# Low-rank and bonus products of an RWKV-7 step in two passes of rounded parts, with the bonus kept in DRAM

## The chip, the cores and the metric

The kernel runs on one core of one Trainium2 chip. The metric is the device time of one execution in microseconds; lower is better. The core has a matmul engine (TensorE, PE), a vector engine (VectorE, DVE), a scalar engine (ScalarE, ACT), GpSimd (POOL) and a sync engine (SyncE, SP) that issues most of the DMAs. Each engine works through its own queue in order and waits on semaphores of the others.

## The reference

One inference step of a hybrid decoder layer, 512 prompt tokens and 8 x 8 sample tokens (576 columns in all), width 1024. RWKV-7 time mixing and differential attention run on the same normalised input, are merged by gates, and a squared-ReLU MLP follows. What matters here is the RWKV branch, 8 heads of 64, cut to the lines that the change computes:

```python
r, k, v, wd, ad, gd = jnp.split(Pr, RWKV_SPLITS, axis=-1)   # wd, ad: 64 wide
w = -jax.nn.softplus(-(lp['w0'] + jnp.tanh(wd) @ lp['w2']).astype(f32)) - 0.5
a = jax.nn.sigmoid((lp['a0'] + ad @ lp['a2']).astype(f32))
g = jax.nn.sigmoid(gd) @ lp['g2']
...
S, y = rwkv7_scan(S0, hs(r), hs(decay), hs(k), hs(v), -kk, kk * hs(a))
...                                                          # y: group norm per head
bonus = jnp.sum(hs(r) * hs(k) * lp['r_k'], axis=-1, keepdims=True) * hs(v)
o = (y + bonus).reshape(B, T, W_A) * g
```

The decay w and the rate a come from products of rank 64 (`w2`, `a2`); the bonus is a sum over the 64 channels of a head, times v.

## The kernel before, in words

Activations lie with channels on the 128 partitions and the 576 tokens along the free axis, split in halves of 288 (`HALF`) for matmuls. Large projections (`stream`) multiply in three passes of rounded parts: the weights and the activations are each split into a rounded high part (an ACT copy to fp32r) and a low part (a DVE subtraction), and high x high, high x low and low x high are summed in PSUM. Their weights come in by SP's queue as tiles `raw_*` (`raw_z` for the RWKV projections, `raw_g` for the gates, `raw_brb`, `raw_bra`, `raw_wo`, `raw_dn` later).

The RWKV projections `shifted(0..13)` give the tiles `Pt[i]`: r, k, v of each of four head pairs hp, then `Pt[12]`, whose lower 64 partitions are wd and upper 64 ad, and `Pt[13]`, gd. After the attention, its pool `ap` closes, and the pools `rb_` and `rt` for the heads open in the space that it leaves. Tiles of the tag "T" in `rt` are 128x576, and six of them exist at a time; a new one waits until one is released.

The generator `rwkv(hp)` does a head pair in stages between its `yield`s:

- Stage 0: `sq`, the squares of k, are summed on PE (`pn`, tiny products), turned into inverse norms on POOL (`nr`, then `nb`), and spread by PE transposes (`pk`). Decay and rate are matmuls `pw` and `pa` of full fp32 operands: `wl` and `al` are 128x512 tiles, zero in the half of the partitions that belongs to the other, so that each multiplies all of `Pt[12]`. ACT empties them by tanh into `u` and `aa`. DVE makes the running sums `cum`, ACT the exponentials `pe`, `pinv`, `pm`. Then come the mixed keys `k2`, `rkp` (r k r_k), the bonus sums `pbn` (an fp32 matmul with a block of ones), `bv` (the bonus times v, a tile of `rb_` with four buffers, kept on chip until the norm), the operands `KB` and `ST`, and the intra-chunk products `pA` with masks (`ABR`, `ST`).
- Stages 1 to 3: transposes, sample states (`s0`, loaded by SP; `pI`), the triangular inverse by 32x32 blocks (`pW`, `pZ`), sample outputs (`pF`). `chain(0)` and `chain(1)` run the nine chunks of two pairs in series (`pch`, `pY`).
- Stage 4: mean and variance of y, the power on POOL. Stage 5: scaling, transposes (`pTy`), `oa` = normed y times weight plus bias, plus `bv`, times the gate `pg`.

Work that fills PE between these steps is taken from a list, `waiting`: the projections of the next pairs (`ps_z`), the gates (`ps_g`), and branch B's output products (`ps_brb`), in amounts written out by hand (`fill(8)`, `take(221)` and so on). `fill` also binds the work to come after the last matmul on PE. Every instruction has a priority, its place in the program unless `prio` gives another, and the order on each queue is planned from these and from when tiles come free; weight loads and their splitting stand ahead of all else (`FEED`). Branch B loads `ob` and `gb` tiles, also of the tag "T"; so are `y2` of the last two pairs and the `g` tiles of the last stage of the branch.

Of the kernel before, what the change touches and what calls it, by code (L numbers as in the profile page):

```python
# [8 lines left out]
F32 = mybir.dt.float32  # L9
F32R = mybir.dt.float32r  # L10
I32 = mybir.dt.int32
AF = mybir.ActivationFunctionType
# [3 lines left out]
P = 128  # L16
# [5 lines left out]
NT = NPR + NS  # L22
# [19 lines left out]
def tile_hybrid_step(ctx, tc, xT, xsT, ktab, vtab, s0T, ptab, w_in, vecs, w2a2, g2, lamv,  # L42
                     w_bra, w_brb, w_out, w_up, w_down, cst, bias_p, bias_s,
                     yT, kTo, vTo, Sp, Ss, sh):
    nc = tc.nc
    PE, VE, AE, GE = nc.tensor, nc.vector, nc.scalar, nc.gpsimd
    PS = bass.MemoryType.PSUM

    def pool(name, bufs=1, stack=ctx, **kw):
        return stack.enter_context(tc.tile_pool(name=name, bufs=bufs, **kw))  # L50

    def f32(ap):
        return ap.bitcast(F32)
# [3 lines left out]
    def act(out, in_, func=AF.Copy, **kw):  # L57
        ring["act"] = AE.activation(out=out, in_=in_, func=func, **kw)  # L58

    def tt(out, a, b, op, eng=None):  # L60
        ins = (eng or VE).tensor_tensor(out=out, in0=a, in1=b, op=op)  # L61
        if eng is None:
            ring["tt"] = ins

    def stt(out, a, s, b, op0, op1):
        VE.scalar_tensor_tensor(out=out, in0=a, scalar=s, in1=b, op0=op0, op1=op1)

    def ts(out, a, s1, op0, s2=None, op1=ALU.bypass, eng=None):
        (eng or VE).tensor_scalar(out=out, in0=a, scalar1=s1, scalar2=s2, op0=op0, op1=op1)

    def mm(out, lhsT, rhs, start=True, stop=True):
        ring["mm"] = PE.matmul(out=out, lhsT=lhsT, rhs=rhs, start=start, stop=stop)  # L72
        return ring["mm"]
# [17 lines left out]
    MUL, ADD, SUB, MAX = ALU.mult, ALU.add, ALU.subtract, ALU.max  # L91
# [9 lines left out]
    def bank(name):  # L101
        return psw.tile([P, 512], F32, tag="w", name=name)

    def tbank(name):
        return psc.tile([P, 512], F32, tag="t", name=name)
# [9 lines left out]
    onesblk = c[:, C_OB:C_OB + P]  # L115
# [13 lines left out]
    up = tbank("warmup")  # L129
# [4 lines left out]
    def v(i, n=1):  # L134
        return vec[:, i:i + n]
# [88 lines left out]
    def fill(n):  # L224

        with tc.issue_after(ring["mm"].ins):
            take(n)
# [12 lines left out]
    def rpow(dst, src, scale, eps):  # L240

        ts(dst, src, scale, MUL, eps, ADD)
        GE.tensor_tensor(out=dst, in0=dst, in1=mhalf[:dst.shape[0], :dst.shape[1]], op=ALU.pow)
# [17 lines left out]
    rc = pool("rc", stack=ph1)  # L261
# [5 lines left out]
    zp = pool("zp", stack=ph1)  # L267
# [3 lines left out]
    with tc.tile_pool(name="xin", bufs=2, reuse_waits="tile") as xin:  # L271
# [6 lines left out]
        for k in range(0, KT, 4):  # L278
            for j in range(3):
                with prio(FEED + 1000 + 10 * k + j):  # L280
                    name = f"raw_{'qkv'[j]}0_{k}"
                    if k == 0:
                        raw = ring["pool"].tile([P, 4, P], F32, tag="raw", name=name, bufs=3)
                    else:
                        raw = zw.tile([P, 1 + NX], F32, tag="z" if j else "tz", name=name,
                                      bufs=2 if j else 1)[:, :4 * P].rearrange("p (k w) -> p k w", k=4)
# [25 lines left out]
    Pt = [None] * 14  # L312
# [5 lines left out]
    ts(ka2[:, 0:4], v(V_KA, 4), 0.5, MUL, 0.0, ADD, GE)  # L318
    ts(ka2[:, 4:8], v(V_KA, 4), -0.5, MUL, 1.0, ADD, GE)

    wl = rc.tile([P, 512], F32, name="wl")
    al = rc.tile([P, 512], F32, name="al")
    GE.memset(wl[64:128], 0.0)
    GE.memset(al[0:64], 0.0)
    wg = rc.tile([P, 512], F32, name="wg")
    reset = rc.tile([P, NT], F32, name="reset")
    GE.memset(reset, 1.0)
# [87 lines left out]
    with tc.issue_after(behind.ins):  # L415
        nc.sync.dma_start(out=pti, in_=ptab)
        nc.sync.dma_start(out=lv, in_=lamv)
        nc.sync.dma_start(out=bp, in_=bias_p)
        nc.sync.dma_start(out=bs, in_=bias_s)
        nc.sync.dma_start(out=wl[0:64], in_=w2a2[0:64])  # L420
        nc.sync.dma_start(out=al[64:128], in_=w2a2[64:128])
        nc.sync.dma_start(out=wg, in_=g2)

    def shifted(i):
# [240 lines left out]
    for h in range(HB):  # L665
        if h:
            qkv(h)
        for cc in range(2):
            GE.tensor_copy(
                out=qbd[64 * cc:64 * cc + 64, :, h, 8 * cc:8 * cc + 8],  # L670
                in_=qT[64 * cc:64 * cc + 64, h, NPR:].rearrange("p (b q) -> p b q", b=NB))
# [11 lines left out]
    while flight:  # L683
        feed()
        fill(8)
    act(Pt[12][0:64], Pt[12][0:64], AF.Tanh)
    sg = Pt[13]
    act(sg, sg, AF.Tanh, scale=0.5)
    ts(sg, sg, 0.5, MUL, 0.5, ADD)
# [25 lines left out]
    rk = ExitStack()  # L715
    rb_ = pool("rb_", 2, stack=rk, reuse_waits="tile")
    rt = pool("rt", 2, stack=rk, reuse_waits="tile")

    def ch(a):
        return a.rearrange("p (c t) -> p c t", t=64)  # L720
# [21 lines left out]
    def rwkv(hp):  # L742
        e = hp % 2
        own = pair.setdefault(hp // 2, {})
        hs = slice(hp * P, (hp + 1) * P)
        r, k, vv = Pt[hp], Pt[4 + hp], Pt[8 + hp]

        def tmp(tag, bufs=1):
            return rt.tile([P, NT], F32, tag="T", name=f"{tag}_{hp}", bufs=6)
# [5 lines left out]
        for t, o in enumerate(toks):  # L755
# [8 lines left out]
                       in_=nr.rearrange("p (a o) -> p a o", o=1).broadcast_to([P, 10, 64]))  # L764
        u = tmp("u")
        aa = tmp("aa")
        for t0, n in HALF:
            pw = bank(f"pw{hp}{t0}")
            mm(pw[:, :n], wl[:, hs], Pt[12][:, t0:t0 + n])
            act(u[:, t0:t0 + n], pw[:, :n], AF.Tanh, scale=0.5, bias=hw0[:, hp:hp + 1])  # L770
            pa = bank(f"pa{hp}{t0}")
            mm(pa[:, :n], al[:, hs], Pt[12][:, t0:t0 + n])
            act(aa[:, t0:t0 + n], pa[:, :n], AF.Tanh, scale=0.5, bias=hw0[:, 4 + hp:5 + hp])
        (fill if hp != 2 else take)(8)
        ts(u, u, 1.0, ADD)
# [25 lines left out]
        tt(k2, k2, k, MUL)  # L801
        rkp = tmp("rkp")
        stt(rkp, r, v(V_RK + hp), k2, MUL, MUL)
        bv = rb_.tile([P, NT], F32, tag="bv", name=f"bv{hp}", bufs=4)
        for t0, n in HALF:
            pbn = bank(f"pbn{hp}{t0}")
            mm(pbn[:, :n], onesblk, rkp[:, t0:t0 + n])
            tt(bv[:, t0:t0 + n], pbn[:, :n], vv[:, t0:t0 + n], MUL)


        KB = rt.tile([P, NCH, 2, 64], F32, tag="KB", name=f"KB{hp}", bufs=1)
# [14 lines left out]
        for par in range(2):  # L826
            rows = slice(64 * par, 64 * par + 64)
# [15 lines left out]
        for cs, pV in two_chunks(f"pV{hp}", vv):  # L843
            for a, c0, c1 in cs:
                src = pV[64 * a:64 * a + 64].rearrange("p (c w) -> p c w", w=P)[:, :(c1 - c0 + 1) // 2]
# [20 lines left out]
        for par in range(2):  # L866
            rows = slice(64 * par, 64 * par + 64)
# [29 lines left out]
        for l in range(1, 5):  # L897

            n = NCH if l < 3 else 8
# [55 lines left out]
        var = stat.tile([P, NCH], F32, tag="var", name=f"var{hp}")  # L955
        VE.tensor_reduce(out=var, in_=y2, axis=AX.X, op=ADD)
        rpow(var, var, 1.0 / 64, 64e-5)

        yield
        tt(y, y, b9(var), MUL)  # L960
# [3 lines left out]
        for cs, pT_ in two_chunks(f"pTy{hp}", y.rearrange("p c t -> p (c t)")):  # L964
            for a, c0, c1 in cs:
                src = pT_[64 * a:64 * a + 64].rearrange("p (c w) -> p c w", w=P)[:, :(c1 - c0 + 1) // 2]
# [78 lines left out]


    gens = [rwkv(hp) for hp in range(4)]

    def run(*stages):
# [254 lines left out]
    rows = []  # L1304
# [10 lines left out]
    for t0, n in LAST:  # L1315
# [55 lines left out]
        w = slice(0, len(tiles))  # L1371
# [133 lines left out]
```

## Time and profile before

| | |
|---|---|
| median of 3 runs | 1001.76 us (1001.45 to 1002.26) |
| profiled execution: span, first to last instruction | 1004.0 us; no other time of it is given |
| busy: PE, DVE, ACT, POOL | 975.5, 689.5, 497.3, 88.3 us |
| share of PE in the chain that ended last | 86% |
| mean granted TensorE clock | 0.989 |

Busy time is the time in which an engine had an instruction at work; a matmul's end is modelled, and matmuls overlap, so their start-to-start distance is what a row of them costs. A row of a timeline gives start, length, engine, line, operation, tile written <- tiles read, shapes and a count. A bracket at its end gives the idle time of that engine before it and what ended it. The head pairs run from about 172 to 522 us.

### The profile page before, as it was taken

Reading aid. Unit: us, or ns where it says so; the run is one execution under the profiler, and the core shown is the slowest. Engines: PE = TensorE matmul, PEld = TensorE weight load, DVE = VectorE, ACT = ScalarE, POOL = GpSimd, SP = SyncE. Lnnn points to the kernel's source line nnn. Section 1 sums busy time; section 2 is a strip of 40 time slices with the busy share of each in tenths; the row PEclk is TensorE's granted clock in tenths of the full one; section 3 lists DMA queues with packets and bytes.
Section 4 is the critical chain, followed back from the end, with each engine's and each line's share of the span. In section 5 each row is a group of like instructions: output and inputs, shape, how many; then the busy total and the mean of one; then the engine's idle time right before and its main releaser. Section 6 shows DMA issues by size and latency. Waiting matters only on the chain.

```text
span 1004.0 us, 24422 instructions
## 1 busy us (share of the span) xinstructions
PE 975.5 (97%) x10012; PEld 919.9 (92%) x10012; DVE 689.5 (69%) x1459; ACT 497.3 (50%) x1094; POOL 88.3 (9%) x171
## 2 busy tenths in 40 slices
PE   8999999899999999999999999999999999999996
PEld 8999998898887878888889999999999999999996
DVE  6698666774946669445588798966666666666744
ACT  6576555354435344443344666644444444444732
POOL 2511001301010340000300000000000000000001
PEclk9999999999989989999999999999999999999998
DMA  7312673121111225222377642222222222221402
GB/s 265 142 66 88 204 221 120 54 64 45 43 47 57 69 87 171 80 70 102 106 215 237 195 152 74 95 85 95 85 85 95 84 85 85 85 84 44 128 10 95
DMA packets 50833, 105.75 MB, mean 105 GB/s; under 512 B 6066, under 2 KB 8114, under 8 KB 50594
## 3 DMA queue, kind: packets, MB, share of 16 engines
q1 hardware_dynamic: 47442, 96.95, 30.2%
q0 software_dynamic: 1648, 5.35, 1.4%
q8 instruction: 79, 1.29, 0.5%
q10 hardware_dynamic: 1632, 1.89, 0.5%
q14 instruction: 32, 0.26, 0.1%
HBM read 89.38 MB, written 14.78 MB: 104 GB/s over the span
## 4 chain that ended last, share of the span: by engine, by line
PE 86%; DVE 6%; ACT 3%; DMA 2%; issue 2%; POOL 1%; SPq 0%; DVEq 0%; POOLq 0%; ACTq 0%
PE ps_dn L72 21%; PE ps_g L72 9%; PE ps_z L72 8%; PE ua L1224 5%; PE ux L1224 5%; PE ps_wo L72 4%; PE uc L1224 3%; PE ud L1224 3%; PE ub L1224 3%; PE ps_k L72 2%; PE ps_brb L72 2%; PE pch L72 2%; PE ps_q L72 2%; PE ps_v L72 2%; PE pA L72 2%
## 5 line engine op out<-in xcount | busy, mean ns | idle before, releaser
L72 PE MATMUL ps_dn<-q,hi_dn 128*128 128x288 f32 x768 | 154.7, 296 | 0.0
L72 PEld LDWEIGHTS ps_dn<-q,hi_dn 128*128 128x128 f32 x768 | 122.8, 188 | 1.5
L72 PE MATMUL ps_dn<-q,lo_dn 128*128 128x288 f32 x384 | 113.2, 295 | 0.0
L72 PE MATMUL ps_g<-xl,hi_g 128*128 128x288 f32 x256 | 80.2, 313 | 0.0
L72 PE MATMUL ps_g<-xh,lo_g 128*128 128x288 f32 x256 | 79.3, 310 | 0.0
L72 PE MATMUL ps_g<-xh,hi_g 128*128 128x288 f32 x256 | 79.2, 310 | 0.0
L72 PEld LDWEIGHTS ps_dn<-q,lo_dn 128*128 128x128 f32 x384 | 72.1, 188 | 0.0
L72 PE MATMUL ps_z<-xh,lo_z 128*128 128x288 f32 (+1 forms) x224 | 69.6, 311 | 0.0
L72 PE MATMUL ps_z<-xh,hi_z 128*128 128x288 f32 (+1 forms) x224 | 68.3, 305 | 0.0
L72 PE MATMUL ps_z<-xl,hi_z 128*128 128x288 f32 (+1 forms) x224 | 67.6, 302 | 0.0
L61 DVE TENSOR_TENSOR ya<-ya,ps_dn 128x288 f32<-128x288 f32 x96 | 43.4, 453 | 29.3 <-PE ps_dn L72 29.3
L58 ACT ACTIVATE hi_dn<-raw_dn 128x512 fp32r<-128x512 f32 x48 | 30.1, 628 | 57.0 <-PE ps_dn L72 57.0
L1224 PE MATMUL ua<-h_b,hi 128*128 128x288 f32 x256 | 53.2, 298 | 0.0
L1224 PE MATMUL ux<-h_t,hi 128*128 128x288 f32 x256 | 52.3, 296 | 0.0
L58 ACT ACTIVATE c<-c 128x288 f32<-128x288 f32 x112 | 48.4, 439 | 7.5 <-DVE c L61 5.8
L72 PEld LDWEIGHTS ps_g<-xh,hi_g 128*128 128x128 f32 x256 | 49.0, 191 | 2.9 <-issue 1.6
L72 PEld LDWEIGHTS ps_g<-xl,hi_g 128*128 128x128 f32 x256 | 49.0, 191 | 1.9
L72 PEld LDWEIGHTS ps_g<-xh,lo_g 128*128 128x128 f32 x256 | 49.1, 192 | 1.4
L58 ACT ACTIVATE hi<-a 128x1024 fp32r<-128x1024 f32 (+1 forms) x32 | 27.1, 846 | 42.0 <-PE ps_dn L72 34.3
L72 PE MATMUL ps_dn<-q,w 128*128 128x320 f32 (+1 forms) x336 | 46.4, 298 | 0.0
L61 DVE TENSOR_TENSOR lo<-s,hi 128x1024 fp32r<-128x1024 f32 x32 | 39.2, 1225 | 10.2 <-ACT hi L58 10.0
L72 PEld LDWEIGHTS ps_dn<-q,w 128*128 128x128 f32 x336 | 45.3, 190 | 0.1
(395 smaller groups left out, 2801.7 us busy)
## 6 DMA issues: line engine op xcount, KB each, us to landing
a<-in_w_up_dram SPq DMA_DIRECT2D x32, 512.0 KB, 3.3
raw_dn<-in_w_down_dram SPq DMA_DIRECT2D x64, 256.0 KB, 2.9
raw_g<-in_w_in_dram SPq DMA_DIRECT2D x32, 256.0 KB, 3.2
raw_z<-in_w_in_dram SPq DMA_DIRECT2D x28, 256.0 KB, 3.0
gt_d<-gg SPq DMA_DIRECT2D x16, 288.0 KB, 2.5
g<-gt_d SPq DMA_DIRECT2D x16, 288.0 KB, 3.7
kp<-in_ktab_dram SPq DMA_DIRECT2D x16, 256.0 KB, 4.0
vp<-in_vtab_dram SPq DMA_DIRECT2D x16, 256.0 KB, 3.7
```

The costliest lines, as they stand in the source:

```text
L58: ring["act"] = AE.activation(out=out, in_=in_, func=func, **kw)
L61: ins = (eng or VE).tensor_tensor(out=out, in0=a, in1=b, op=op)
L72: ring["mm"] = PE.matmul(out=out, lhsT=lhsT, rhs=rhs, start=start, stop=stop)
L1224: ring["mm"] = PE.matmul(out=ps[:, :288], lhsT=l[:, k], rhs=hb[blk][:, h, k], start=start and i == 0, stop=i == 11, skip_group_check=skip)
```

## The change

The low-rank products and the bonus sums are made of rounded parts in two passes each.

- One tile `wa` holds both weights, w2 on partitions 0 to 63 and a2 on 64 to 127; `wl`, `al` and their two memsets go, and two DMAs become one.
- After the pools `rb_` and `rt` open, the weights of each are rounded to `hi` (twice, into both halves of the partitions) and the remainder goes to `lo` (also into both). `stacked` puts the rounded activation on the rows of its own half and its remainder on the other half's, so that one pass with `hi` gives high x high plus high x low, and a second with `lo` adds low x high (and low x low). `xa` is made of ad; the tanh of wd, before done in place after the projection, goes to a tile `th` here, and `xw` is made of that.
- `pw` and `pa` become two fp32r matmuls each (`lowrank`).
- `rkp` is split into `rkh` (ACT) and `rkl` (DVE), and the bonus sum is two fp32r matmuls with `ones2`, a rounded copy of the block of ones.
- `bv` becomes a tile of the tag "T", is written to DRAM (`bv_d`) by SP's queue, and read back (`bvl`) at the end of stage 4.

```diff
-    wl = rc.tile([P, 512], F32, name="wl")
-    al = rc.tile([P, 512], F32, name="al")
-    GE.memset(wl[64:128], 0.0)
-    GE.memset(al[0:64], 0.0)
+    wa = rc.tile([P, 512], F32, name="wa")
...
-        nc.sync.dma_start(out=wl[0:64], in_=w2a2[0:64])
-        nc.sync.dma_start(out=al[64:128], in_=w2a2[64:128])
+        nc.sync.dma_start(out=wa, in_=w2a2)
...
-    act(Pt[12][0:64], Pt[12][0:64], AF.Tanh)
     sg = Pt[13]
...
+    bv_d = tc.dram_tile([4, P, NT], F32, name="bv_d")
+    ones2 = rb_.tile([P, P], F32R, name="ones2", bufs=1)
+    act(ones2, onesblk)
+
+    def stacked(pool_, name, src, rows, tag=None):
+        up, dn = rows, slice(64 - rows.start, 128 - rows.start)
+        x = pool_.tile([P, NT], F32R, tag=tag or name, name=name, bufs=1)
+        act(x[up], src[up])
+        tt(x[dn], src[up], f32(x[up]), SUB)
+        return x
+
+    lo_, up_ = slice(0, 64), slice(64, 128)
+    low = []
+    for name, rows in (("w", lo_), ("a", up_)):
+        hi = rb_.tile([P, 512], F32R, name=f"{name}h", bufs=1)
+        lo = rb_.tile([P, 512], F32R, name=f"{name}l", bufs=1)
+        for half in (lo_, up_):
+            act(hi[half], wa[rows])
+        for half in (lo_, up_):
+            tt(lo[half], wa[rows], f32(hi[rows]), SUB)
+        low.append((hi, lo))
+    xa = stacked(rb_, "xa", Pt[12], up_)
+    th = rt.tile([P, NT], F32, tag="T", name="th", bufs=6)
+    act(th[lo_], Pt[12][lo_], AF.Tanh)
+    Pt[12] = None
+    xw = stacked(zp, "xw", th, lo_, "P12")
+
+    def lowrank(ps, which, hs, x, t0, n):
+        hi, lo = low[which]
+        mm(ps[:, :n], hi[:, hs], x[:, t0:t0 + n], stop=False)
+        mm(ps[:, :n], lo[:, hs], x[:, t0:t0 + n], start=False)
...
-            mm(pw[:, :n], wl[:, hs], Pt[12][:, t0:t0 + n])
+            lowrank(pw, 0, hs, xw, t0, n)
...
-            mm(pa[:, :n], al[:, hs], Pt[12][:, t0:t0 + n])
+            lowrank(pa, 1, hs, xa, t0, n)
...
-        bv = rb_.tile([P, NT], F32, tag="bv", name=f"bv{hp}", bufs=4)
+        rkh = rt.tile([P, NT], F32R, tag="T", name=f"rkh_{hp}", bufs=6)
+        act(rkh, rkp)
+        rkl = rt.tile([P, NT], F32R, tag="T", name=f"rkl_{hp}", bufs=6)
+        tt(rkl, rkp, f32(rkh), SUB)
+        bv = tmp("bv")
         for t0, n in HALF:
             pbn = bank(f"pbn{hp}{t0}")
-            mm(pbn[:, :n], onesblk, rkp[:, t0:t0 + n])
+            mm(pbn[:, :n], ones2, rkh[:, t0:t0 + n], stop=False)
+            mm(pbn[:, :n], ones2, rkl[:, t0:t0 + n], start=False)
             tt(bv[:, t0:t0 + n], pbn[:, :n], vv[:, t0:t0 + n], MUL)
+        nc.sync.dma_start(out=bv_d[hp], in_=bv)
...
         rpow(var, var, 1.0 / 64, 64e-5)
+        bv = tmp("bvl")
+        nc.sync.dma_start(out=bv, in_=bv_d[hp])
 
         yield
         tt(y, y, b9(var), MUL)
```

## The prediction

> **What bounds the kernel now.** I read the page's busy times and chain first, then the stretches in which the four head pairs start, then the tiles that the change touches, and last the order of time around them.
>
> ```profile
> PE 975.5 (97%) x10012; PEld 919.9 (92%) x10012; DVE 689.5 (69%) x1459; ACT 497.3 (50%) x1094; POOL 88.3 (9%) x171
> PE 86%; DVE 6%; ACT 3%; DMA 2%; issue 2%; POOL 1%; SPq 0%; DVEq 0%; POOLq 0%; ACTq 0%
> 178.60:182.20 3.60, 0.93 (x9) 0.69 (x7) 1.87 (x3) 1.25 (x2) 3.45 (x8) 1.00 0.00 0
> 182.20:185.60 3.40, 3.40 (x16) 3.40 (x15) 3.00 (x7) 1.21 (x2) 3.17 (x6) 0.51 0.00 0
> 250.60:261.00 10.40, 10.10 (x76) 9.85 (x74) 10.11 (x19) 4.53 (x7) 0.00 (x0) 1.00 0.17 52
> 277.80:281.20 3.40, 3.40 (x81) 2.58 (x81) 1.24 (x5) 0.82 (x3) 1.95 (x1) 0.51 0.00 0
> 281.20:284.60 3.40, 3.40 (x81) 3.12 (x81) 1.64 (x2) 1.04 (x2) 0.72 (x1) 0.50 0.02 5
> 366.60:370.00 3.40, 3.40 (x17) 3.40 (x17) 0.60 (x2) 1.21 (x6) 1.23 (x1) 0.50 0.01 2
> 370.00:373.40 3.40, 3.40 (x10) 2.07 (x9) 1.88 (x5) 2.17 (x4) 2.67 (x3) 0.50 0.22 77
> 373.40:386.50 13.10, 12.31 (x92) 11.93 (x91) 12.22 (x22) 6.55 (x12) 3.20 (x6) 1.00 0.30 95
> 490.00:507.00 17.00, 16.18 (x105) 13.03 (x104) 12.26 (x23) 4.71 (x9) 7.82 (x7) 1.00 0.50 166
> ```
>
> The span is 1004.0 us, 2.2 above the median of the runs, 1001.76; the profiled execution has no other time beside it, so I work in differences within this execution and take them off the median. In the rows of stretches the columns after the length are the busy time of PE, PEld, DVE, ACT and POOL, then the granted clock, the DMA share and GB/s. The reader is to see three things. PE carries 86% of the chain, so a shorter PE program shortens the kernel wherever PE doesn't then wait. Where a head pair starts, DVE is as full as PE (10.11 of 10.40 us, 12.22 of 13.10). And five stretches of 3.4 us ran at half clock, all at starts of head pairs: 17 us that cost some 8.5.
>
> **The change, part by part.**
>
> *PE passes.* The products of the low ranks and of the bonus lose fp32 operands.
>
> ```profile
> 175.50 0.30 PE L72 MATMUL ps_z<-xh,lo_z 128*128 128x288 f32 x1
> 175.63 0.30 PE L72 MATMUL ps_z<-xh,hi_z 128*128 128x288 f32 x1
> 175.77 0.65 PE L72 MATMUL pw<-P,wl 128*128 128x288 f32 x2
> 176.25 0.65 PE L72 MATMUL pa<-P,al 128*128 128x288 f32 x2
> 176.74 0.65 PE L72 MATMUL pw<-P,wl 128*128 128x288 f32 x2
> 177.22 0.65 PE L72 MATMUL pa<-P,al 128*128 128x288 f32 x2
> 177.84 0.29 PE L72 MATMUL ps_z<-xh,lo_z 128*128 128x288 f32 x1
> L72 PE MATMUL pbn<-rkp,cst_sb x16: 403/406/510, 193.8 to 387.4; 128*128 128x288 f32 x16
> 370.34 1.16 PE L72 MATMUL pw<-P,wl 128*128 128x288 f32 x2
> 371.30 1.17 PE L72 MATMUL pa<-P,al 128*128 128x288 f32 x2
> ```
>
> Start to start counts, not the duration, since matmuls overlap. An fp32 product is two records and takes 0.485 us (176.25 - 175.77, 176.74 - 176.25 and so on). A product of rounded parts, as ps_z, starts every 0.133. The new form needs two of those, 0.267, so each of the 24 products (per head pair two for the decay, two for a, two for the bonus) gives 0.218: 5.2 us in all, 0.87 + 0.44 per pair. The Trainium skill, "FP8 and Floating Point Precision", section "TensorE Precision Notes", counts four passes for true fp32. Four of this trace's 0.133 would be 0.53 a product and 6.4 us saved, an estimate; the trace has 0.485, and that is used.
>
> What reaches the path differs by pair. Pair 0, decay and a: nothing, because PE then waits for POOL anyway:
>
> ```profile
> 178.64 0.30 PE L72 MATMUL ps_z<-xh,lo_z 128*128 128x296 f32 x1
> 172.68 0.76 ACT L58 ACTIVATE sq<-P,vec 128x576 f32<-128x576 f32 x1
> 173.49 1.28 PE L72 MATMUL pn<-cst_sb,sq 128*128 128x2 f32 x10
> 176.29 2.16 POOL L818 MEMSET ST<- 64x1152 f32 x2
> 178.43 2.18 POOL L760 TENSOR_TENSOR nr<-nr,mhalf 128x10 f32<-128x10 f32 x1
> 180.85 0.71 POOL L763 COPY nb<-nr 128x640 f32<-128x640 f32 x1
> 181.61 0.66 PE L76 MATMUL pk<-cst_sb,nb 128*128 128x128 f32 x4 [2.67 <-POOL nb L763]
> 176.94 0.50 ACT L58 ACTIVATE aa<-pa,hw 128x288 f32<-128x288 f32 x1
> ```
>
> Pair 1: 0.6 of the 0.87, since ACT empties the banks at 0.50 us each and would now be slower than PE. Pair 2: 0.87. Pair 3 runs at half clock up to 373.4 (0.96 a product, 371.30 - 370.34): three at 0.96 and one at 0.485, 3.4 us, become 3 x 0.53 + 0.27 = 1.9, but ACT needs 4 x 0.50 = 2.0, so 1.4 (at full clock throughout, 0.87). Bonus: 4 x 0.44 = 1.75. Together **-4.6**; the ends are -5.2 (all of it) and -1.75 (only the bonus reaches the path).
>
> *Preparation of the stacked parts.* Once, ahead of pair 0.
>
> ```profile
> L58 ACT ACTIVATE ks<-kT 64x512 fp32r<-64x512 f32 x16 | 10.0, 628 | 1.5 <-PE pss L72 1.3
> L61 DVE TENSOR_TENSOR lo_z<-raw_z,hi_z 128x512 fp32r<-128x512 f32 x28 | 19.3, 690 | 10.8 <-ACT hi_z L58 6.5 <-PE pq L72 3.3 <-PE ps_z L72 0.2
> L58 ACT ACTIVATE obh<-ob x4: 674/684/685, 389.9 to 392.7; 128x576 fp32r<-128x576 f32 x4
> L61 DVE TENSOR_TENSOR obh<-ob,obh x4: 720/753/754, 392.2 to 405.3; 128x576 fp32r<-128x576 f32 x4
> 165.00:178.60 13.60, 13.26 (x127) 11.93 (x120) 5.60 (x21) 7.11 (x15) 4.83 (x7) 1.00 0.33 107
> ```
>
> ACT: four roundings of 64x512 at 0.63, three of 64x576 at 0.68 (xa, xw, and the tanh, which moves here from before), ones2 some 0.3: 4.9 us. DVE: four differences at 0.69 and two at 0.75: 4.3 us. No row shows 64x576 parts; I use the 128-row ones. The cover is there: ACT is busy 7.1 and DVE 5.6 of 13.6 us. What isn't covered: these stand in program order ahead of sq, in pools whose space the attention tiles leave only here. If all of ACT's 4.9 us goes ahead of sq (172.68), pn runs at 178.3 instead of 173.49, ends at 179.6, and nr, 2.18 of POOL and 0.71 of nb give pk at 183.1 instead of 181.61: +1.5, not +4.9, because POOL was held by its memset until 178.45 anyway. Queued behind the late pn on PE are the fill products, pw and pa. Bounds 0 and +1.5; I take **+0.5**, nearer to 0 because ACT has free time there.
>
> *Per pair: rkh on ACT (0.68), rkl on DVE (0.75).* ACT is free over half of these stretches: nothing; without that cover 4 x 0.68 = 2.7. DVE is not free: 4 x 0.75 = 3.0 at most. rkl delays only the bonus product itself, which nothing but bv needs; it reaches PE through the DVE queue, where the KB and ST parts that pA needs and the low halves of the fill's weights stand behind it. Bounds 0 and +3.0; I take **+1.0**, since PE has fill to run meanwhile in three of four pairs and the queue is full in all.
>
> *bonus times v through DRAM.* Four stores and four loads of 288 KB on SP's queue, and bv, rkh, rkl and the reloaded tile share six buffers "T" with the loads for branch B.
>
> ```profile
> gt_d<-gg SPq DMA_DIRECT2D x16, 288.0 KB, 2.5
> g<-gt_d SPq DMA_DIRECT2D x16, 288.0 KB, 3.7
> L478 SPq DMA_DIRECT2D gb<-gt_d x8: 320/371/456, 391.2 to 512.7; - x8
> 360.03 5.13 DMA s<-in_s0T_dram
> ```
>
> Eight issues of about 0.35 on a queue that is mostly idle, 2.5 us a store, 3.7 a load, at DMA shares of 0.17 to 0.5: hidden behind the tens of microseconds between norm and use. The store waits for DVE's bv, and weight loads queue behind it; but DVE is at work on bv when the store is put there, so the wait is short. The s load that PE waited for (5.13 us on the chain) waits for its buffer, not for SP, so the store isn't in its way. A reloaded tile holds a buffer from the variance to the sum with oa, so a gb or g load near 495 to 520 can come one buffer later. If the cover is gone, one load, 3.7. Bounds 0 and +3.7; I take **+0.3**.
>
> *Removed at the start:* two POOL memsets and one DMA issue: 0; POOL works 88.3 us in all.
>
> Sum: -4.6 + 0.5 + 1.0 + 0.3 = **-2.8 us**, 1001.8 - 2.8 = 999.0.
>
> **The rivals.**
>
> *The fill runs out at the norm.* What PE saves at pairs 0 to 3 pulls fill forward, and it is missing where the last two pairs wait for mean, variance and POOL's power (490 to 507, PE already idle 0.8 us of 17). Then the 4.6 us come back as idle PE time there: 1001.5 at the small costs that remain. Against it: from 507 on the chain is PE work again:
>
> ```profile
> 507.06 2.26 PE ps_brb L72 x15
> ```
>
> *DVE becomes the bound: slower.* Place: the starts of the pairs. Price: 4.3 + 3.0 = 7.3 us of added DVE work, all on the path because the KB, ST and mask operations behind it already run back to back. It decides from 6.6 (4.6 + 2.0) on. Then -4.6 + 7.3 = +2.7: 1004.5. For it: 10.11 of 10.40; against it: pair 2 runs between the steps of the serial chain, where DVE has gaps, and the 4.3 may fall before 172.
>
> *The clock, dearer.* The rows show half clock after the 2.97 us gap (178.64 to 181.61). If PE stands still from 173.5 to 178.3 for the late sq, one more 3.4 us stretch at half clock costs 1.7: 1000.7. The Trainium skill, "TensorE: Matmul & The Clock Gate", Part 1, says that an idle window of about 3.4 us halves the clock, and that the window runs free. By that rule, a gap of 4.9 us makes it likely and one of 3 a matter of phase; the trace agrees at 182.2, but at 277.8 and 366.6 the clock fell with PE nearly busy, on small products.
>
> *The clock, cheaper.* The two long half-clock stretches (277.8 to 284.6, 366.6 to 373.4) each cost 3.4. If the shifted work avoids one, 999.0 - 3.4 = 995.6. Nothing speaks for it but that the stretches depend on what falls together.
>
> **How the numbers follow.** The sum, 999.0: 0.43. Cheaper clock, 995.6: 0.10. Fill runs out, 1001.5: 0.14. Dearer clock, 1000.7: 0.10. DVE bound, 1004.5: 0.23. 0.2% is 2.0 us, about what this measurement can tell from no change. Faster 0.53 (first two), same 0.24, slower 0.23. The unknown costs reach from -5.2 - 1.7 = -6.9 (994.9) to -4.6 + 1.5 + 1.7 + 3.0 + 3.7 = +5.3 (1007.1), all mishaps together; the range 995.0 to 1004.5 takes in every case's time and leaves about 2 in 10 outside. The likeliest case alone has 997.0 to 1000.0.
>
> **What would show it.** Right: pw, pa and pbn as 128x288 records at 0.133 start to start, PE's busy time some 5 us less; pn a few microseconds later but pk near 182; rkl in the DVE queue beside KB and ST, with pbn behind pA; stores of bv_d landing in 2.5 us and reloads long before oa. Wrong: fp32 products paced by ACT so that nothing is gained; pk past 183.5; pA later after rkp than before by more than rkl's 0.75; gaps of PE over 1 us at 495 to 535 with a DMA as releaser; other than five stretches of half clock.

## The result, and the profile after

The change made the kernel slower: 1016.5 us median (1011.6 to 1018.5, five executions) against 1001.5 us for the kernel before. The ratio is 1.0143, 95% interval 1.0127 to 1.0158; a second comparison gave 1.0156 (1.0136 to 1.0176). That is 15 us lost where 2.8 were to be gained, far outside the range 995.0 to 1004.5.

The profiled execution of after is the fastest of its five (span 1009.7 us, 1011.6 us in all); that of before, shown above, was slow for its kind. A second profile of the unchanged kernel (below) has a span of 997.3 us, 999.1 in all. It is used for comparisons from here on, called "before, second profile"; the two executions of one program differ in how often PE ran at half clock, five stretches of 3.4 us ahead of 990 us in the first and two in the second.

The page of after, busy times and chain, then the same two lines of before, second profile:

```profile
PE 973.6 (96%) x10012; PEld 920.1 (91%) x10012; DVE 698.0 (69%) x1469; ACT 503.0 (50%) x1105; POOL 86.8 (9%) x169
PE 84%; DVE 7%; ACT 4%; issue 2%; POOL 2%; DMA 1%; SPq 0%; DVEq 0%; POOLq 0%; ACTq 0%
```

```profile
PE 970.5 (97%) x10012; PEld 916.4 (92%) x10012; DVE 688.4 (69%) x1459; ACT 497.3 (50%) x1094; POOL 88.1 (9%) x171
PE 84%; DVE 7%; ACT 4%; DMA 2%; issue 2%; POOL 1%; SPq 0%; DVEq 0%; ACTq 0%; POOLq 0%
```

PE has 84% of the chain in both, so these shares say nothing of the loss; the 86% ahead of the prediction belong to that execution. PE is busy 3.1 us longer in after, and without work for 36.1 us instead of 26.8 (1009.7 - 973.6, 997.3 - 970.5). What is wait and what is half clock is read from one stretch, from 165 us to the first `ps_wo` matmul, which holds the same stages in each kernel. First before, second profile, then after; columns are length, busy PE, PEld, DVE, ACT, POOL with counts, granted clock, DMA share, GB/s. Below it the stretches at half clock and their sums.

```profile
165.00:545.70 380.70, 367.69 (x5289) 326.68 (x5280) 253.88 (x568) 167.16 (x385) 51.31 (x81) 0.99 0.30 98
...
182.50:185.90 3.40, 3.40 (x16) 3.40 (x15) 2.83 (x7) 1.79 (x3) 3.17 (x8) 0.50 0.00 0
278.00:281.40 3.40, 3.40 (x82) 3.23 (x81) 0.45 (x2) 1.05 (x3) 2.67 (x2) 0.51 0.02 5
```

```profile
165.00:556.80 391.80, 370.65 (x5295) 330.67 (x5296) 263.73 (x581) 173.84 (x397) 51.01 (x81) 0.97 0.31 102
...
175.70:185.90 10.20, 8.22 (x34) 7.92 (x34) 5.14 (x10) 4.53 (x8) 9.57 (x18) 0.50 0.12 37
284.90:291.70 6.80, 5.34 (x90) 4.60 (x89) 4.52 (x12) 2.83 (x6) 2.61 (x2) 0.50 0.01 2
377.10:380.50 3.40, 3.40 (x24) 3.06 (x22) 1.80 (x3) 2.97 (x7) 3.23 (x3) 0.51 0.23 79
```

The stretch grew by 11.1 us. Idle time of PE (length less busy) went from 13.0 to 21.2, +8.1. PE's busy time at half clock went from 6.8 to 17.0; half of it is lost, 3.4 and 8.5, +5.1. What remains, PE's work counted at full clock, went from 364.3 to 362.2, -2.1. So some PE work was saved, and waits and half clock took several times as much.

How much half clock takes depends on the execution. In before's first profile the same stretch has 386.70 us, 372.43 busy, 17.0 of it at half clock; against that one after has 6.9 us more idle time, no more at half clock, and 1.8 less work. Over all timed executions the mean clock is 0.992 before and 0.983 after (table below).

Where PE waits in after, in order of time, with what kept it:

```profile
173.14 1.26 ACT L58 ACTIVATE wh<-wa 64x512 fp32r<-64x512 f32 x2
174.42 1.27 ACT L58 ACTIVATE ah<-wa 64x512 fp32r<-64x512 f32 x2
175.59 0.66 ACT L58 ACTIVATE xa<-P 64x576 fp32r<-64x576 f32 x1
176.28 0.68 ACT L58 ACTIVATE th<-P 64x576 f32<-64x576 f32 x1
176.87 0.76 ACT L58 ACTIVATE sq<-P,vec 128x576 f32<-128x576 f32 x1
177.68 2.29 PE L72 MATMUL pn<-cst_sb,sq 128*128 128x2 f32 x10 [3.79 <-ACT sq L58]
180.01 0.17 DVE L69 TENSOR_SCALAR nr<-pn 128x10 f32<-128x10 f32 x1 [1.11 <-PE pn L72]
180.59 2.17 POOL L851 MEMSET ST<- 64x1152 f32 x2
183.00 1.99 POOL L787 TENSOR_TENSOR nr<-nr,mhalf 128x10 f32<-128x10 f32 x1
185.44 0.72 POOL L790 COPY nb<-nr 128x640 f32<-128x640 f32 x1
186.22 0.66 PE L76 MATMUL pk<-cst_sb,nb 128*128 128x128 f32 x4 [0.25 <-POOL nb L790]
...
251.06 0.29 PE L72 MATMUL pw<-xw,wh 128*128 128x288 f32 x1
251.19 0.29 PE L72 MATMUL pw<-xw,wl 128*128 128x288 f32 x1
252.89 0.41 PE L72 MATMUL pa<-xa,ah 128*128 128x288 f32 x1 [0.46 <-ACT u L58]
...
287.63 0.69 PE L76 MATMUL pk<-cst_sb,nb 128*128 128x128 f32 x2 [1.46 <-POOL nb L790]
...
351.39 3.04 POOL L61 TENSOR_TENSOR vm<-SVU,cst_sb 128x512 f32<-128x512 f32 x3
351.42 3.56 DVE L61 TENSOR_TENSOR lo_g<-raw_g,hi_g 128x512 fp32r<-128x512 f32 x1
358.03 1.13 PE L72 MATMUL pA<-ST,KB 128*128 128x128 f32 x8 [2.12 <-DVE ST L61]
...
397.56 0.53 PE L72 MATMUL pbn<-rkh,ones 128*128 128x288 f32 x2 [1.44 <-ACT rkh L58]
```

Pair 0: the whole preparation stands on ACT ahead of `sq`; PE stands still and then runs `pn` at half clock (2.29 us, 1.28 before); the late `nr` finds POOL at a second memset of ST; `pk` starts at 186.22 instead of 181.61. By `pn` of pair 1, which starts at 247.39 instead of 241.87, 5.5 us are lost. Pair 1: the products wait 0.46 us for ACT to empty a bank, as in before (0.48 in its second profile). Pair 2: the products are through sooner, and `pk` waits 1.46 us for POOL's `nb`; before has this `pk` at another place of PE's queue, at 304.46. At 351.42 a DVE subtraction that takes 0.68 us elsewhere takes 3.56, and `pA` of pair 2 waits behind it. Pair 3: `pbn` waits 1.44 us for ACT's `rkh`, where before waits 1.82 for `rkp`. At pair 0 the wait moved from `pk` (2.67 us in before) to `pn` (3.79); the two at pair 2 are new.

### The profile page after: what moved, and what is told of

Same layout as the page of the kernel before. It is cut to its first block, busy times and chain, and to the rows that moved or that the text cites. A ratio compares the mean times of both kernels' runs of the same rounds, so it can differ in the third digit from the quotient of the medians.

```text
span 1009.7 us, 24451 instructions
## 1 busy us (share of the span) xinstructions
PE 973.6 (96%) x10012; PEld 920.1 (91%) x10012; DVE 698.0 (69%) x1469; ACT 503.0 (50%) x1105; POOL 86.8 (9%) x169
## 4 chain that ended last, share of the span: by engine, by line
PE 84%; DVE 7%; ACT 4%; issue 2%; POOL 2%; DMA 1%; SPq 0%; DVEq 0%; POOLq 0%; ACTq 0%
PE ps_dn L72 20%; PE ps_g L72 9%; PE ps_z L72 8%; PE ua L1259 5%; PE ux L1259 5%; PE ps_wo L72 4%; PE uc L1259 3%; PE ud L1259 3%; PE ub L1259 3%; PE ps_bra L72 3%; PE ps_k L72 2%; PE ps_brb L72 2%; PE pch L72 2%; PE ps_q L72 2%; PE ps_v L72 2%
```

## The experiments

Two kinds of cause were open: the work that the change adds on ACT, DVE and the DMAs, or the order on the queues, planned anew, and what follows from it (waits, collisions, the clock). The letters that the expectations give to theories hold within each of them. Differences in us are against the kernel before, as ratio less one times 1001.

| kernel | what it is | difference | 95% interval of the ratio | mean clock |
|---|---|---|---|---|
| after_again | the change | +15.6 | 1.0136 to 1.0176 | 0.983 |
| prep_late | preparation behind `sq`, `pn`, `nr` of pair 0 | +10.0 | 1.0082 to 1.0119 | 0.985 |
| lowrank_dram | bonus as before, bv in DRAM | +9.6 | 1.0078 to 1.0114 | 0.986 |
| bonus_only | low ranks as before | +5.7 | 1.0038 to 1.0076 | 0.989 |
| after_dummy | 24 idle matmuls ahead of `pn` | +16.5 | 1.0151 to 1.0179 | 0.984 |
| bonus_chip | bonus in two passes, bv on chip | +6.4 | 1.0051 to 1.0078 | 0.991 |
| dram_only | only bv in DRAM | +4.3 | 1.0029 to 1.0056 | 0.992 |
| bonus_pad | bonus_only, T buffers where they lay | +4.3 | 1.0029 to 1.0057 | 0.993 |
| before_vmact | before, `vm` on ACT | +0.5 | 0.9993 to 1.0017 | 0.992 |
| dram_vmact | dram_only, `vm` on ACT | +0.9 | 0.9997 to 1.0021 | 0.994 |
| after_vmact | the change, `vm` on ACT | +13.6 | 1.0115 to 1.0158 | 0.983 |
| late_vmact | prep_late, `vm` on ACT | +9.2 | 1.0074 to 1.0109 | 0.987 |
| nosplit_vmact | after_vmact, no split of rkp | +11.2 | 1.0096 to 1.0128 | 0.983 |
| noprep_vmact | after_vmact, little preparation | +12.1 | 1.0104 to 1.0139 | 0.984 |
| none_vmact | both left out | +8.8 | 1.0071 to 1.0104 | 0.985 |
| late_none | both left out, and late | +6.8 | 1.0054 to 1.0083 | 0.986 |
| pad_vmact | bonus_pad, `vm` on ACT | +2.1 | 1.0009 to 1.0033 | 0.991 |

The kernel before had a mean clock of 0.992 or 0.993 in each comparison. Each kernel was timed at least five times.

**Halves of the change.** after_again is the changed kernel once more, bonus_only has the old low ranks, lowrank_dram the old bonus product:

```diff
 # bonus_only: wl, al, their memsets and DMAs are back
-            lowrank(pw, 0, hs, xw, t0, n)
+            mm(pw[:, :n], wl[:, hs], Pt[12][:, t0:t0 + n])
 ...
 # lowrank_dram: ones2, rkh and rkl go
 ...
-            mm(pbn[:, :n], ones2, rkh[:, t0:t0 + n], stop=False)
-            mm(pbn[:, :n], ones2, rkl[:, t0:t0 + n], start=False)
+            mm(pbn[:, :n], onesblk, rkp[:, t0:t0 + n])
 # prep_late: the block from ones2 to xw moves into rwkv(0), behind nb
+        if hp == 0:
+            ones2 = ...
+            ...
+            xw = stacked(zp, "xw", th, lo_, "P12")
```

> The changed kernel once more, for its spread and its clock beside the kernel before. Theory S (the start: the preparation stands ahead of sq on ACT, so pn, nr and pk of pair 0 come some 4.6 us later and PE's first fill runs at half clock): +5 to +15 us in every execution, sq at 176 to 177 us. Theory D (DVE: rkl and the preparation lengthen a full DVE queue): the loss is spread over the starts of pairs 1 and 3 instead, and pair 0 holds less than a third of it. Theory C (clock: the phase of the half-clock windows decides): times scatter by more than 5 us and follow the mean granted clock, about 1 us per 0.001.

> The bonus in two passes and bv through DRAM, but decay and a as before in fp32 with no preparation. S: the start of pair 0 is back at 172.7 for sq and the time is within 3 us of before, below it by up to 1.7 (the bonus passes). D: rkl is still there, so about half of the loss stays, +5 to +8. C: no statement by itself, the scatter stays if the shift of work does it.

> Decay and a in two passes with the preparation as in the change; the bonus in fp32 with no rkh and rkl, bv through DRAM. S: the loss stays nearly whole, +5 to +15. D: the loss falls by the part of rkl, to +3 to +8, and the starts of pairs 1 to 3 look as before.

> The whole change, but the preparation stands in the program behind sq, pn and the inverse norm of pair 0 instead of ahead of them. S: sq returns to 172.7, pk to about 181.6 and the time falls by 4 us or more against the change as it was. D: DVE has the same work, so the time stays within 2 us of the change as it was.

Each half by itself is slower than before, so neither hides a gain of the other. The place of the preparation in the program is worth 5.6 of the change's 15.6, with the queues planned anew for it. `sq` returned to 172.5, but `pk` came at 184.25 and not near 181.6: `pw`, ahead of it in PE's queue, waited 4.48 us for `xw`. `pn` of pair 1 starts 2.0 us sooner than in after (245.44 against 247.39), so more than half of the 5.6 comes behind the start.

The other expectations decide less. after_again fits theory S nearly (+15.6, expected 5 to 15) and has the sign of theory C as well: its five times spread over 7.2 us, from 1012.6 at a clock of 0.987 to 1019.8 at 0.978, though all are over 10 us above before. bonus_only lies where theory D had it, but its `sq` did not return to 172.7, for a reason shown below. lowrank_dram lies in the range of S and above that of D.

**The start, and the clock there.** after_dummy fills the first wait of PE with dead matmuls, so that `pn` runs at full clock; nothing else moves:

```diff
+    idle = tbank("idle")
+    with tc.issue_after(ring["mm"].ins if hasattr(ring["mm"], "ins") else ring["mm"]):
+        for _ in range(24):
+            mm(idle[:, :288], xh[:, 0, :P], xh[:, 0, :288])
```

> The change with 24 matmuls of no use (128x288, rounded operands, their result is read by nothing) put on PE in front of pn of pair 0, where PE waits 3.8 us for sq; the order of all five queues is otherwise the same. Theory C (a good part of the loss is half clock, started by the standing PE): the half-clock stretch of 10.2 us at 175 to 186 shortens, the mean clock rises by 0.002 or more and the time falls by 2 to 5 us. Theory S (only the wait itself counts): the 24 take 3.2 us of a wait of 3.8 and the time stays within 1 us.

`pn` took 1.3 us again, but `pk` came at 186.1 as before the filling: POOL's queue, not PE, was last. The time did not fall. So the wait ahead of `pn` was not what cost time. The price of half clock is not told by this run: near the start two spans of 3.4 us stayed at half clock (from 179.8 and 186.6; after and after_again have three and two), and the mean clock, 0.984, did not rise.

**The bonus part by part.** dram_only changes no product at all; bonus_chip keeps bv on chip; bonus_pad adds a filler to `rb_` so that the T buffers get their old addresses:

```diff
 # dram_only, against before
-        bv = rb_.tile([P, NT], F32, tag="bv", name=f"bv{hp}", bufs=4)
+        bv = tmp("bv")
 ...
+        nc.sync.dma_start(out=bv_d[hp], in_=bv)
 # bonus_pad, against bonus_only
+    pad = rb_.tile([P, 2176], F32, name="pad", bufs=1)
+    GE.memset(pad[0:32, 0:1], 0.0)
```

> As bonus_only, with a tile of 8.5 KB that nothing uses in the place that the four bv tiles left, so that the tiles of the tag T lie again where they lay before; the order of the queues is the same as in bonus_only but for one small memset. Theory O (sq of pair 0 waits because its buffer now lies over osT, an attention tile that DVE reads until 176): sq returns to about 172.7, pk to 181.6 and the time falls by 2 us or more against bonus_only. Against it (the wait is for something else): within 1 us of bonus_only.

> The kernel before with nothing changed but bv: a tile of the tag T, written to DRAM and read back at the norm; all products in fp32. If DRAM and the shared T buffers cost: +2 us or more, of which the place of sq's buffer (as in bonus_only) is up to 3. If they are hidden as forecast: within 1 us of before, or up to +3 with sq waiting for osT.

> The kernel before with only the bonus in two passes (ones2, rkh, rkl), bv on chip in its four buffers. Theory D (DVE is the bound at the starts of the pairs): +1 to +3 us for rkl in spite of the 1.7 us that PE saves. As forecast (+1.0 for rkl, -1.75 for PE): -2 to 0 us. If the change of plan that comes with it costs more than the work: over +3 us.

dram_only was the surprise: +4.3 us with no added work on PE, DVE or ACT. bonus_chip, with neither DRAM nor bv in the T buffers, has +6.4, more than rkl was expected to cost; that case was expected only if the change of plan costs more than the work. The queues show why dram_only needn't lose by its DMAs: in the traces some 300 of the 10012 matmuls and some 50 of the 1459 DVE instructions stand at another place than in before, since other buffers are free at other times. For one, `pk` of pair 2 starts at 282.12 instead of 306.92. And bonus_only against bonus_pad shows the addresses at work, in the first `sq`. The timeline of ACT in bonus_only, then in bonus_pad:

```profile
176.02 0.77 ACT L58 ACTIVATE sq<-P,vec 128x576 f32<-128x576 f32 x1 [2.28 <-DVE obs L66]
```

```profile
172.75 0.76 ACT L58 ACTIVATE sq<-P,vec 128x576 f32<-128x576 f32 x1
```

With bv gone from `rb_`, the buffer of `sq` lies where the attention's last tile still is in use, and `sq` waits for `obs`, its last reader. The filler removes that wait (1.4 us by the two ratios, whose intervals overlap; 2 us or more were expected).

**The stall beside POOL.** All the changed kernels so far, after and the first eight of the table, have one long DVE operation at pair 2 that before doesn't have: 3.56 or 3.57 us, in bonus_only and bonus_pad 3.92. dram_only's timeline (DVE, POOL, PE), then before's first profile at the same place, then bonus_pad's:

```profile
345.18 3.04 POOL L61 TENSOR_TENSOR vm<-SVU,cst_sb 128x512 f32<-128x512 f32 x3
345.21 3.56 DVE L61 TENSOR_TENSOR lo_g<-raw_g,hi_g 128x512 fp32r<-128x512 f32 x1
348.28 2.16 POOL L821 MEMSET ST<- 64x1152 f32 x2
348.80 0.75 DVE L66 SCALAR_TENSOR_TENSOR ST<-sq,u 64x576 f32<-64x576 f32 x1
351.81 1.13 PE L72 MATMUL pA<-ST,KB 128*128 128x128 f32 x8 [2.15 <-DVE ST L61]
```

```profile
344.27 0.68 DVE L61 TENSOR_TENSOR lo_g<-raw_g,hi_g 128x512 fp32r<-128x512 f32 x1
...
345.85 0.76 DVE L61 TENSOR_TENSOR ST<-P,pe 64x576 f32<-64x576 f32 x1
345.97 3.56 POOL L61 TENSOR_TENSOR vm<-SVU,cst_sb 128x512 f32<-128x512 f32 x3
346.64 0.68 DVE L61 TENSOR_TENSOR ABR<-pA,cst_sb 64x512 f32<-64x512 f32 x1
348.65 1.05 PE L72 MATMUL pA<-ST,KB 128*128 128x128 f32 x8
```

```profile
348.71 3.92 DVE L66 SCALAR_TENSOR_TENSOR ST<-sq,u 64x576 f32<-64x576 f32 x1
348.97 3.04 POOL L61 TENSOR_TENSOR vm<-SVU,cst_sb 128x512 f32<-128x512 f32 x3
```

In dram_only `lo_g` reads two tiles in SBUF and starts 0.03 us behind POOL's first `vm`; it ends 0.55 us after the third one (345.18 + 3.04 = 348.22), nearly its own 0.68 us. In before the order was the other: `ST`, also with two tiles in SBUF, came first, POOL took 3.56 us instead of 3.04, and the DVE operations behind it, which read `pA` in PSUM, ran at their usual 0.68 beside POOL. Beside POOL's memset, which reads nothing, the `ST` at 348.80 takes its usual 0.75. The Trainium skill, "SBUF — State Buffer", section "Who interferes with whom", says this: a DVE instruction with two SBUF inputs contends with a GpSimd instruction that reads SBUF, the later one is blocked, and one that only writes does no harm. The trace agrees for `lo_g`, for `ST` and POOL in before, for the operations that read PSUM and for the memset. The rows of bonus_pad do not fit the order of starts: there `ST` starts 0.26 us ahead of `vm` and still takes 3.92 us, while `vm` keeps its 3.04. Which of the two is held up when they start that close is not settled here.

The test moves `vm` of pairs 0 and 1 to ACT and leaves all else; PE's queue differs in 2 places, DVE's in at most 14:

```diff
+            if hp < 2:
+                for b in range(NB):
+                    act(vm[:, b], SVU[:, 8, par], scale=c[:, C_MB + b:C_MB + b + 1])
+            else:
                 tt(vm, m3(SVU[:, 8, par], NB), ..., MUL, GE)
```

> The kernel before with the four masked products vm of pairs 0 and 1 (ahead of pF) made by ACT, eight small copies with a scale each, instead of POOL; the order on the other queues stays the same but for a few places. It is the control for the two kernels that follow. In the profile of before no DVE operation was held up beside POOL's vm (345.97 to 349.53): its DVE operations there had their usual 0.68 to 0.76 us. Theory S (a DVE operation with two operands in SBUF stands still while POOL works on vm): nothing to gain here, 0 to +1 us against before. Rival T (vm on ACT is simply better or worse than on POOL, whatever DVE does): the same change as in the next two kernels.

> The kernel with nothing of the change but bv in DRAM (dram_only, +4.8 us against before), with vm of pairs 0 and 1 on ACT. Theory S: in dram_only lo_g took 3.56 us instead of 0.68 at 345.2 because POOL's vm ran beside it, ST and pA of pair 2 stood behind it on DVE, and that is all of the +4.8: now lo_g has 0.68 us, pA of pair 2 takes about 7 us instead of 10.6, and the time is 0 to 1.5 us above before. Rival P (the PE order, which was planned anew, or the waits for the loads of bvl cost the 4.8): +3.5 to +5.5 as in dram_only.

> The whole change, with vm of pairs 0 and 1 on ACT. Theory S: 4 to 5 us less than the change (+15 against before), so +10 to +11.5. Rival P: +14 to +16.

> The kernel before once more, for a second profile of it: the first had a span of 1004.0 us, 2 to 6 us more than its timed executions. If the stretches at half clock come and go between executions, this one has others than the five of the first ahead of 990 us, and its span is nearer to 999; if they belong to the kernel, the same five.

dram_vmact, DVE and PE:

```profile
343.82 0.68 DVE L61 TENSOR_TENSOR lo_g<-raw_g,hi_g 128x512 fp32r<-128x512 f32 x1
344.53 0.76 DVE L66 SCALAR_TENSOR_TENSOR ST<-sq,u 64x576 f32<-64x576 f32 x1
...
348.12 1.05 PE L72 MATMUL pA<-ST,KB 128*128 128x128 f32 x8
```

The stall is gone and with it 3.4 of the 4.3 us of dram_only; the control did not move. So most of the loss of dram_only is that stall: a collision, brought about by the new order. In the whole change the same edit gave only 0.7 to 2.0 us (from +14.3 or +15.6 to +13.6, intervals overlapping); the expected 4 to 5 did not come.

**The added work.** The next four take away the preparation's place, the split of rkp, the preparation of the weights, and the last two together. In nosplit_vmact the product writes `rkh` itself, which is used in both passes; in noprep_vmact each weight is loaded into both halves and rounded once, and used in both passes.

```diff
 # nosplit_vmact
 ...
-        stt(rkp, r, v(V_RK + hp), k2, MUL, MUL)
-        act(rkh, rkp)
-        tt(rkl, rkp, f32(rkh), SUB)
+        stt(rkh, r, v(V_RK + hp), k2, MUL, MUL)
 ...
 # noprep_vmact
 ...
-        for half in (lo_, up_):
-            act(hi[half], wa[rows])
-        for half in (lo_, up_):
-            tt(lo[half], wa[rows], f32(hi[rows]), SUB)
-        low.append((hi, lo))
+        act(hi, src)
+        low.append((hi, hi))
```

> The whole change with the preparation after sq, pn and nr of pair 0, and vm of pairs 0 and 1 on ACT. If the two costs are separate, it has both gains: 4.6 us from the place of the preparation and about 2 from vm, so +7 to +9 us against before. If the gain of vm was only given back elsewhere, +10 to +11.

> The whole change with vm of pairs 0 and 1 on ACT; the split of rkp is left out: rkh is written by the product itself and stands in for rkl in the second pass, so that ACT's rkh and DVE's rkl (8 operations) are gone and PE's work is the same. Theory D (DVE and ACT at the starts of the pairs are the cost of the bonus, 3 us of rkl and its wait): 3 to 5 us less than after_vmact (+13.5), so +8.5 to +10.5. Rival C (the clock and the order on PE, whatever DVE does): +12 to +15.

> The whole change with vm of pairs 0 and 1 on ACT; the preparation of the weights is left out but for two roundings: each of the two weights is loaded into both halves of the partitions, rounded by one ACT copy, and the same rounded tile stands in for the low part, so that two ACT copies and four DVE differences are gone. xa, th and xw stay. Theory D: pk of pair 0 some 3 us earlier and the time 3 to 5 us less than after_vmact, +8.5 to +10.5. Rival C: +12 to +15.

> Both left out: the split of rkp and the preparation of the weights, with vm of pairs 0 and 1 on ACT. PE's passes are those of the change. If the added DVE and ACT work at its two places and the stall beside POOL are the whole cause, nothing is left but the saved passes and xa, xw: +1 to +5 us against before. If the order and the clock cost something of their own, +8 or more is left.

Moving the preparation gave 4.4 us (13.6 to 9.2) here too, as expected. Leaving out the split gave 2.4 and the preparation 1.5, each less than the 3 to 5 expected if the added work were the cause (the intervals against after_vmact overlap or touch); both together 4.8. With that work gone, 8.8 us remain, as expected only if the order and the clock cost something of their own. So this work, with the order that comes with it, is about a third of the loss; two roundings, `xa`, `th` and `xw` are still there.

The last two take the start out of what remains, and look at the bonus alone without stall and overlap. late_none is prep_late with the edits above; pad_vmact is bonus_pad with `vm` on ACT.

> Everything at once: the two-pass products of the change with the split of rkp and the preparation of the weights left out (as in none_vmact, +9.4), vm of pairs 0 and 1 on ACT, and what is left of the preparation (two roundings, xa, th, xw) after sq, pn and nr of pair 0, so that sq doesn't wait for the attention's last tile (it began at 175.9 in none_vmact and at 172.6 in before). Theory W (PE's saved work of 3 to 4 us is spent in waits and at half clock, of which 3 to 4.6 us lie at the start): +4.5 to +6.5 us against before. If the start alone were what is left of the loss: -1 to +3. If its place doesn't matter: +9.

> The bonus alone in two passes, with bv in DRAM, a filler tile in rb_ that keeps the T buffers where they lay before (bonus_pad, +4.5), and vm of pairs 0 and 1 on ACT. In bonus_pad a DVE operation on ST took 3.92 us instead of 0.75 beside POOL's vm. If that stall was the loss: 0 to +1.5 us against before, and the 1.75 us of saved passes show or not at that size; if the rkl on DVE costs 3 by itself, +3 or more.

pad_vmact: two passes of the bonus, with split and DRAM, cost 2.1 us (0.9 to 3.3) once the stall is gone; that lies between the two cases expected and decides for neither. late_none: +6.8 (5.4 to 8.3), near the 4.5 to 6.5 of theory W and far above -1 to +3, although `sq`, `pk` of pair 0 and `pn` of pair 1 now start at 172.5, 181.7 and 242.0, where they started at 172.6, 181.5 and 241.9 in before's second profile. So the rest of the loss is behind the start. Its stretch from 165, and the spans of 3.4 us where before, second profile, has its own at half clock:

```profile
165.00:552.50 387.50, 370.39 (x5287) 330.24 (x5279) 255.58 (x569) 177.72 (x423) 47.86 (x77) 0.97 0.32 103
...
176.00:179.40 3.40, 1.67 (x7) 1.70 (x8) 0.77 (x2) 1.50 (x3) 3.30 (x4) 0.50 0.17 42
179.40:182.80 3.40, 3.40 (x17) 3.38 (x17) 2.06 (x3) 1.12 (x3) 3.16 (x10) 0.50 0.00 0
275.00:278.40 3.40, 2.50 (x47) 2.33 (x46) 1.08 (x3) 2.76 (x9) 0.00 (x0) 1.00 0.00 0
278.40:281.80 3.40, 2.06 (x8) 1.69 (x8) 2.50 (x7) 1.96 (x4) 3.05 (x2) 0.50 0.00 0
281.80:285.20 3.40, 3.31 (x81) 2.92 (x82) 2.15 (x3) 0.52 (x2) 0.04 (x1) 0.50 0.02 5
```

and before, second profile, at the same place:

```profile
274.60:278.00 3.40, 2.78 (x44) 2.43 (x44) 3.27 (x10) 2.55 (x8) 0.00 (x0) 1.00 0.00 0
278.00:281.40 3.40, 3.40 (x82) 3.23 (x81) 0.45 (x2) 1.05 (x3) 2.67 (x2) 0.51 0.02 5
281.40:284.80 3.40, 3.40 (x157) 2.99 (x156) 1.77 (x4) 0.73 (x2) 0.00 (x0) 0.99 0.22 77
```

PE's idle time is 17.1 us here against 13.0, and it has four stretches at half clock (two of them double), 20.5 us with 17.3 us of work, against two; its work at full clock is 2.6 less (361.7 against 364.3). +4.1 + 5.3 - 2.6 = +6.8. Read the six rows in pairs: in both kernels the span up to 278 has small products and waits (2.50 and 2.78 us busy) and the next one is at half clock. In before that one is full of work, and the clock returns at 281.4. In late_none it holds eight passes and a wait for `pk`, 2.06 us busy, and the next one is at half clock too. dram_vmact has the four fp32 products at this place, with `pk` right behind them, and fills the span. Its stretch from 165, that span, and the next:

```profile
165.00:550.00 385.00, 370.35 (x5285) 327.04 (x5277) 254.73 (x567) 175.12 (x417) 47.52 (x77) 0.99 0.32 103
...
277.80:281.20 3.40, 3.35 (x9) 1.96 (x8) 3.29 (x9) 1.85 (x4) 2.94 (x2) 0.50 0.00 0
281.20:284.60 3.40, 3.40 (x159) 2.99 (x157) 2.65 (x6) 1.41 (x4) 0.00 (x0) 1.00 0.02 5
```

But a full span does not always bring the clock back. In before's first profile (277.80 to 284.60, among the rows of the prediction) PE was busy for all 3.40 us and the next span was at half clock too; the profiles of before_vmact and pad_vmact have the same at 276.2 and 278.6, all three with the low-rank products in fp32.

Nor do single profiles place the 6.8 us. Against dram_vmact, which has two spans at half clock with 6.75 us of work, late_none's stretch is 2.5 us longer: 2.5 more idle, 5.3 more for half clock, and 5.2 less work at full clock. Up to `pn` of pair 3 the two are level (366.56 in both; 363.28 in before's second profile), so what late_none loses against dram_vmact comes behind that. PE's work at full clock, by the same count, is 363.9 to 367.0 in the five profiles of kernels whose products are all as in before, so this count has 3 us of play. By the ratios late_none loses 5.9 us to dram_vmact.

## Why the prediction was wrong, step by step

*PE passes, -4.6.* The passes came as forecast, two records per product at 0.133 us at full clock (251.06 to 251.19). What failed is "what reaches the path". Pair 1: the second `pa` starts at 252.89, 0.56 us behind ACT's first `u`, and in before's second profile at 247.36, 0.55 behind it; ACT sets the pace in both, so the forecast 0.6 of 0.87 is nothing. Pair 2: the products are sooner through, and `pk` waits for POOL's `nb`: 1.9 us start to start from the last product to `pk` (280.02 to 281.89 in late_none), where dram_vmact with its fp32 products has 0.7. The saved 0.87 became a wait. The prediction had said this of pair 0 alone, and it took the order on PE's queue as given: in before, second profile, `pk` of pair 2 comes 27 us behind the first product (277.40 and 304.46), in the change directly behind the products. Over the whole stretch PE's work is 2.1 us less than in before's second profile and 5.2 less in late_none than in dram_vmact, which has this `pk` at the same place: the work went about as forecast, the time did not follow.

*Preparation, +0.5 of 0 to 1.5.* Wrong, and outside its bounds: moving it in the program gives 4.4 to 5.6 us. The bound's first half was right: all of ACT's work went ahead of `sq`, and `pn` came at 177.68 (the bound had 178.3). The second half was not: "POOL was held by its memset" was put down as cover, and it was assumed that POOL would be free by the time `nr` came. Another memset (180.59, 2.17 us) went in front, `pn` itself ran at half clock (+1.0, without effect by after_dummy), and `pk` came at 186.22 instead of the bound's 183.1. The sign "pk past 183.5" was met.

*rkh, rkl, +1.0 of 0 to 3.0; DRAM and T buffers, +0.3 of 0 to 3.7.* Together the bonus forecast was -1.75 + 1.3, about zero; without the stall it measured +2.1 (pad_vmact), inside the bounds. DRAM alone is +0.9 (dram_vmact), also inside. As built, dram_only measured +4.3, outside: the prediction priced the DMAs and buffers and not what another order on the queues can run into, the stall of 3 us beside POOL. No rival had it, although the trace of before shows POOL's `vm` and DVE side by side at 346, and a place on the DVE queue decides.

*Rivals.* "DVE becomes the bound" had the right sign, but its mechanism is not what was shown: with rkl and the differences of the weights gone 8.8 us remain. "The clock, dearer" was right in kind, priced at one stretch (1.7 us); after has 17.0 us of PE's work at half clock against 6.8. Its place, pair 0, holds two of the four spans that after has more, but filling the wait there brought no gain (after_dummy). The gap that this rival starts from is 2.67 us by the bracket of its row, not 2.97. The fill did not run out: PE's waits ahead of `ps_brb` are 0.52 and 0.54 us in after, 0.52 twice in before's second profile.

*What is shown and what is not.* In medians: the stall 1 to 2 us, the place of the preparation 4.4, the work of preparation and split some 2.4 (late_vmact less late_none, intervals overlapping), and 6.8 that remain of 15. For these 6.8 the cause stays open; what the profiles show is more idle time and more half clock. All kernels with the two-pass low ranks have a mean clock of 0.983 to 0.987, all without them 0.989 to 0.994 (the table); 0.0064 of 1004 us are 6.4 us between late_none and before, an upper bound, since half clock in a wait costs nothing. That thinner work on PE around waits for POOL and ACT keeps the clock down longer fits the rows of late_none and dram_vmact, does not explain the full spans of before, and was not tested: no kernel held PE's density and the number of passes apart. Nor was the low-rank part run alone with `vm` on ACT. No kernel tried beats before.

## What to carry to other kernels

A pass saved on PE is worth nothing where PE next waits for another engine's result, as at pairs 1 and 2 here; look at every place where saved time would land for the wait that then becomes visible, and for what it does to the granted clock. When a change moves buffers, ask what the queues will do in a new order: here storing one tile elsewhere cost more than the work that it brought. A DVE operation with two tiles in SBUF beside a POOL operation that reads SBUF is a collision worth looking for in the trace of before, as it may be missed there by as little as the 0.12 us here (345.85 to 345.97).

## What the runs showed of the hardware that was not expected

- A DVE subtraction of 0.68 us took 3.56, and a scaled product of 0.75 took 3.92, beside three of POOL's `vm` in a row (3.04 us); with a PSUM operand DVE kept its 0.68 us. POOL took 3.56 us instead when DVE was 0.12 us ahead, but not when it was 0.26 ahead.
- At pair 2 the clock fell to half after spans of 3.4 us in which PE was busy 2.50 us (late_none), 2.78 (before, second profile) and 3.08 (dram_vmact, 274.4 to 277.8), mostly on small products, and with no single wait over 1 us. It stayed at half after spans with 2.06 us busy (late_none) and with all 3.40 (before, first profile). The Trainium skill, "TensorE: Matmul & The Clock Gate", Part 1, has in its table of the two states an idle window of about 3.4 us ahead of the fall; in these rows 0.3 to 0.9 us without work was enough.
